# Four feed-forward layers of a model on one core: mixer outputs in the order 0, 4, 1, 5, ..., the seven products reordered, two token factors made inside the first pair

## The chip, the core and the metric

The kernel runs on one core of a Trainium2 chip. The core has a matrix engine (TensorE, "PE" in the profile; its weight loads are listed apart as "PEld"), a vector engine (VectorE, "DVE"), a scalar engine (ScalarE, "ACT"), a general engine (GpSimd, "POOL") and an engine that only issues transfers here (SyncE, "SP"). Each engine runs its own queue of instructions strictly from front to back; an instruction that waits for a semaphore holds up everything behind it in its queue. The metric is the device time of one execution in microseconds (us).

## The reference, cut to what matters

A block of four layers works on 512 tokens of width 1024, in float32. Each layer is a mixer (two state-space and gated-linear-attention halves, a latent attention, a retention, a stick-breaking attention) and then a feed-forward part with a hidden width of 2816 (22 x 128):

```python
x = x + mixer(rms_norm(x, mix_norm))            # four different mixers
x = x + swiglu(rms_norm(x, ffn_norm), w_gate, w_up, w_down)

def swiglu(h, w_gate, w_up, w_down):
    return (jax.nn.silu(h @ w_gate) * (h @ w_up)) @ w_down

def rms_norm(x, w):
    y = x * lax.rsqrt(jnp.mean(x * x, axis=-1, keepdims=True) + 1e-6)
    return y * w
```

The change touches the place where a mixer's output is added to x and the gate and up products of the following feed-forward part begin. There are four such places. They are called the first to the fourth place here.

## The kernel before, in words

x lies in SBUF transposed, as eight tiles of 128 features x 512 tokens, numbered m = 0 to 7. A float32 product is made of three passes: each operand is split into a high part rounded to the engine's fp32r type and a low remainder (`hh`/`hl` for x, `oh`/`ol` for combinations of x, `wh`/`wl` for weights), and high x high, high x low and low x high are accumulated in PSUM. The high part is made by ACT, the low part by DVE.

A mixer ends with its output projection. It makes one output tile m after the other in PSUM (`lin`), and `residual` adds it to tile m of x on DVE and then calls `norm_prep` for the next layer. The first and the third mixer use `out_a` (24 matmuls of 512 columns for each output and one weight piece of 128 x 1024), the second and the fourth `out_two` (12 matmuls for each output; one weight piece serves two outputs). Before the change the outputs come in the order 0, 1, ..., 7.

The feed-forward part computes gate and up with seven products in place of eight. The four weight blocks are b11, b12, b21, b22 (up and gate, for the tiles 0 to 3 and the tiles 4 to 7 of x), and the tokens are cut into two halves of 256. Product n multiplies one weight factor with one token factor (`self.opers[n]`, four entries k = 0 to 3, one for each tile of 128 features). Token factor 1 is the first half of the tiles 0 to 3, factors 2 and 3 are the two halves of the tiles 4 to 7; the factors 4 to 7 are sums and differences of these, so entry k of them needs tile k and tile k + 4. `operand` (line 433) makes them: for m below 4 a copy of x times the gain (`xg`) and the split; for m from 4 on another copy `xg`, four combinations `xo` of 256 columns on DVE (L210, L219), four roundings `oh` of 256 columns on ACT (L226) and four remainders `ol` of 256 columns on DVE. `norm_sq` squares the tile on ACT and adds it to a running sum `sq`, on POOL, or on DVE for m = 7.

`pair_seven` (line 625) then makes one pair of hidden tiles: seven products of 24 matmuls of 256 columns each (`seven`, line 612), in the order 1, 5, 6, 4, 2, 3, 7, and the additions, the scaling with the norm's factors `rbc` and the SiLU between them. It runs 11 times in each feed-forward part. The weight factors in the same order are b11, a = b11 + b12, a + b22, d = b12 + b22, b21, a + b21 (+ b22), b22. `wsum` makes a sum while it is loaded: SP loads one block into a buffer `ws`, and POOL issues a second transfer that adds the other block to it; a further block is added by DVE in place (`ws<-ws,wr`). Each of the three weight tags (`wr`, `ws` and the converted `wh`/`wl`) has three buffers of 128 x 1024. The norm's sum over features (a matmul with ones, then a Newton iteration on DVE in `ry`, `ra`, `rv`) and its broadcast (a matmul with `ident`) stand in a small queue `vq` that `fill` empties every other group of matmuls, so they fall among the first products of the first pair.

The code only says what depends on what and in which order it was written. The framework's scheduler fixes each engine's order when the program is built, and may put instructions of a later product between those of an earlier one. The order on each engine is therefore part of the change.

## Time and profile before

| what | value |
|---|---|
| median of 3 runs | 2796.18 us (2795.95 to 2799.39) |
| profiled execution | 2799.2 us, span of its trace 2797.1 us |
| PE busy | 98% of the span |
| DVE busy | 67% |
| ACT busy | 43% |
| POOL busy | 9% |
| mean granted clock of PE | 0.987 |
| data read from memory | 309.77 MB, 112 GB/s over the span |

PE is busy nearly all the time; the stretches where it is not, and those where its granted clock is below 1, are short. The profile's second part cuts the span into 40 slices and shows both: all slices have PE at 8 tenths or more, and the mean hides what happens within a slice of 70 us. The timeline and the sums over chosen stretches are needed for that.

### The profile page before, as it was taken

What the parts mean: (1) busy time and instruction counts of PE and PEld (TensorE: products, weight loads), DVE (VectorE), ACT (ScalarE), POOL (GpSimd) and SP (SyncE); (2) the same over time, 40 slices, a digit from 0 to 9 for tenths busy, and PEclk for the clock granted to TensorE, in tenths of its full rate; (3) what the DMA queues carried; (4) which work ended last, traced back from release to release, by engine and by line L of the source; (5) the groups of instructions that cost most, each with busy time, mean ns of one, the idle gap of its engine ahead of it and who ended that gap; (6) DMA issues with size and microseconds to landing.
All of it is one profiled execution on the core that took longest, in us unless ns stands there. A gap on an engine that the chain in (4) does not pass through costs nothing.

```text
span 2797.1 us, 40184 instructions
## 1 busy us (share of the span) xinstructions
PE 2729.5 (98%) x15989; PEld 2348.3 (84%) x15989; DVE 1873.2 (67%) x3020; ACT 1211.7 (43%) x1893; POOL 243.9 (9%) x230
## 2 busy tenths in 40 slices
PE   8999998999998999999999999999999999899999
PEld 6787768999876679998888888799988877699987
DVE  7466567888349977887345544678864388888852
ACT  5444334445226664444233333444442365644431
POOL 2011001000002110000000000100001011100000
PEclk9999998999999998999999999999999999999999
DMA  6232213766321115674332222267643211157632
GB/s 201 86 107 91 68 55 92 191 175 178 96 82 43 46 38 150 176 190 134 98 111 78 87 84 79 80 155 193 169 134 100 91 55 52 46 146 185 168 112 77
DMA packets 91739, 314.50 MB, mean 112 GB/s; under 512 B 10320, under 2 KB 12176, under 8 KB 91552
## 3 DMA queue, kind: packets, MB, share of 16 engines
q1 hardware_dynamic: 78880, 265.79, 29.6%
q0 software_dynamic: 12672, 46.14, 10.3%
q8 instruction: 126, 2.06, 0.3%
q14 instruction: 61, 0.50, 0.1%
HBM read 309.77 MB, written 2.13 MB: 112 GB/s over the span
## 4 chain that ended last, share of the span: by engine, by line
PE 60%; DVE 4%; ACT 1%; issue 1%; POOL 0%; DVEq 0%; ACTq 0%; POOLq 0%
PE lin L229 45%; PE mx L229 14%; PE mx L233 1%; DVE P L1503 1%; DVE wl L210 1%; DVE beta L210 0%; ACT wh L226 0%; DVE hl L219 0%; DVE xo L210 0%; DVE ol L210 0%; DVE x L210 0%; DVE ws L210 0%; POOL sq L210 0%; DVE xo L219 0%; ACT oh L226 0%
## 5 line engine op out<-in xcount | busy, mean ns | idle before, releaser
L226 ACT ACTIVATE wh<-wr 128x1024 fp32r<-128x1024 f32 (+2 forms) x411 | 423.0, 1033 | 824.5 <-PE lin L229 391.6
L210 DVE TENSOR_TENSOR wl<-wr,wh 128x1024 fp32r<-128x1024 f32 (+2 forms) x411 | 491.8, 1198 | 415.9 <-ACT wh L226 415.1
L229 PE MATMUL lin<-hh,wh 128*128 128x512 f32 (+1 forms) x1432 | 491.0, 344 | 7.4 <-ACT wh L226 7.3
L229 PE MATMUL lin<-hl,wh 128*128 128x512 f32 (+1 forms) x1432 | 486.6, 340 | 0.8 <-DVE hl L219 0.8
L229 PE MATMUL lin<-hh,wl 128*128 128x512 f32 (+1 forms) x1432 | 485.6, 339 | 0.8 <-DVE wl L210 0.8
L229 PE MATMUL lin<-oh,wh 128*128 128x256 f32 x1056 | 306.2, 290 | 23.8 <-ACT oh L226 23.5
L229 PE MATMUL lin<-ol,wh 128*128 128x256 f32 x1056 | 306.1, 290 | 4.8 <-DVE ol L210 4.6
L229 PEld LDWEIGHTS lin<-hh,wh 128*128 128x128 f32 x1432 | 271.6, 190 | 43.6 <-issue 7.6
L229 PE MATMUL lin<-oh,wl 128*128 128x256 f32 x1056 | 305.1, 289 | 0.4 <-DVE wl L210 0.3
L229 PEld LDWEIGHTS lin<-hl,wh 128*128 128x128 f32 x1432 | 271.6, 190 | 31.9 <-DVE hl L219 3.5
L229 PEld LDWEIGHTS lin<-hh,wl 128*128 128x128 f32 x1432 | 271.5, 190 | 32.0 <-DVE wl L210 2.0
L226 ACT ACTIVATE wh<-ws 128x1024 fp32r<-128x1024 f32 x176 | 185.6, 1056 | 253.4 <-DVE ws L210 126.2
L229 PE MATMUL lin<-fh,wh 128*128 128x512 f32 x704 | 274.3, 390 | 0.0
L229 PE MATMUL lin<-fl,wh 128*128 128x512 f32 x704 | 273.9, 389 | 0.0
L229 PE MATMUL lin<-fh,wl 128*128 128x512 f32 x704 | 273.8, 390 | 0.0
L229 PEld LDWEIGHTS lin<-oh,wh 128*128 128x128 f32 x1056 | 207.8, 197 | 27.1 <-ACT oh L226 26.9
L210 DVE TENSOR_TENSOR wl<-ws,wh 128x1024 fp32r<-128x1024 f32 x176 | 215.1, 1224 | 21.9 <-ACT wh L226 21.9
L229 PE MATMUL lin<-wh,hh 128*128 128x512 f32 (+1 forms) x560 | 224.8, 402 | 0.8 <-ACT v L226 0.7
L229 PE MATMUL lin<-wh,hl 128*128 128x512 f32 (+1 forms) x560 | 217.7, 389 | 0.0
L229 PE MATMUL lin<-wl,hh 128*128 128x512 f32 (+1 forms) x560 | 216.7, 387 | 0.0
L229 PEld LDWEIGHTS lin<-ol,wh 128*128 128x128 f32 x1056 | 208.5, 197 | 6.7 <-DVE ol L210 6.7
L229 PEld LDWEIGHTS lin<-oh,wl 128*128 128x128 f32 x1056 | 208.7, 198 | 1.1 <-DVE wl L210 1.0
(297 smaller groups left out, 4967.6 us busy)
## 6 DMA issues: line engine op xcount, KB each, us to landing
wr<-in_wgu_dram SPq DMA_DIRECT2D x132, 512.0 KB, 4.3
ws<-in_wgu_dram SPq DMA_DIRECT2D x88, 512.0 KB, 4.3
ws<-in_wgu_dram POOLq DMA_DIRECT2D x88, 512.0 KB, 7.4
wr<-in_wd_dram SPq DMA_DIRECT2D x64, 512.0 KB, 3.6
wr<-in_wo_dram SPq DMA_DIRECT2D x48, 512.0 KB, 3.5
wr<-in_w3b_dram SPq DMA_DIRECT2D x32, 512.0 KB, 3.5
wr<-in_w1b_dram SPq DMA_DIRECT2D x24, 512.0 KB, 3.7
wr<-in_wd_dram SPq DMA_DIRECT2D x32, 384.0 KB, 3.2
```

What stands on the lines that cost most here:

```text
L210: (eng or self.nc.vector).tensor_tensor(out=out, in0=a, in1=b, op=op)
L226: self.nc.scalar.activation(out, a, f, **k)
L229: self.last = self.nc.tensor.matmul(out, lhsT, rhs, start=start, stop=stop, **k)
L233: self.nc.tensor.transpose(out, in_, self.ident[0:n, 0:n])
L1503: self.nc.vector.tensor_tensor_scan(P[:, 0:ke - 1][:, ::-1], d, d, 1.0, op0=ALU.mult, op1=ALU.bypass)
```

## The change

Three things change together. First, all mixers write their outputs in the order of `PAIRS`, and the weight pieces are loaded (and for `out_two` packed) in that order, so tile k + 4 follows tile k at once. Second, `operand` builds the factors otherwise. The copy `xg` is made for m below 4 only. Factors 4 and 5 are made in one tile of 512 columns, with one rounding `oh` and one remainder `ol` for both; their signs are turned, and the additions in `pair_seven` become subtractions. Factors 6 and 7 are made the same way by a function `late`: in the first and the third feed-forward part (`EARLY`) at once, but for m = 7, and else inside the first pair, behind products 1 and 4. Third, the products run in the order 1, 4, 2, 5, 6, 3, 7, with the weight factors in the order b11, d, b21, a, a + b22, a + b22 + b21, b22; the transfers of a summed factor are issued one job ahead (`joblist`). The copy of product 1 (`u2`) now stands between products 1 and 2, which accumulate into the same PSUM tile X. Product 6's tile Y moves from the pool `lin` (3 buffers) to the pool `mx` (5 buffers). The norm's sum is written behind product 5 and its broadcast behind product 3 of the first pair.

```diff
+PAIRS = (0, 4, 1, 5, 2, 6, 3, 7)
+EARLY = ("ffn1", "ffn3")
...
-                yield from (A["wo1"][i, m] for i in range(2) for m in range(8))
+                yield from (A["wo1"][i, m] for i in range(2) for m in PAIRS)
...
-        return [first, second, third, fourth, lambda: st["b21"], lambda: (st["a"], None, plus("b21")),
-                lambda: st["b22"]]
+        return [(put("b11", lambda: self.wraw(b11)), None),
+                (lambda: (st["d"], None, None), put("d", lambda: self.wsum(b12, b22))),
+                (put("b21", lambda: self.wraw(b21)), None),
+                (lambda: (st["a"], None, None), put("a", lambda: self.wsum(b11, b12))),
+                (fifth, None),
+                (lambda: (st["a"], None, plus("b21")), None),
+                (lambda: st["b22"], None)]
...
     def operand(self, m, gain):
+        if m == 0:
+            self.opers = {n: [None] * 4 for n in range(1, 8)}
+            self.xas, self.late = [None] * 4, deque()
+        k = m % 4
+        x, g = self.x[:, m, :], self.col(gain, m)
         own = lambda o: tuple(a[:, o:o + 256] for a in self.h[m])
...
+        def halves(t, n, scale):
+            hi, lo = [self.T2(F32R, name=f) for f in ("oh", "ol")]
+            self.act(hi, t, AF.Copy, scale=scale)
+            self.stt(lo, t, scale, hi.bitcast(F32), ALU.mult, ALU.subtract)
+            for i in range(2):
+                self.opers[n + i][k] = tuple(a[:, 256 * i:256 * i + 256] for a in (hi, lo))
+
         if m < 4:
...
-            def parts(n):
-                if k % 2 == 0:
-                    self.ot[n] = [self.T2(F32R, name=f) for f in ("oh", "ol")]
-                hi, lo = [a[:, 256 * (k % 2):256 * (k % 2) + 256] for a in self.ot[n]]
-                self.act(hi, o[n], AF.Copy)
-                self.tt(lo, o[n], hi.bitcast(F32), ALU.subtract)
-                self.opers[n].append((hi, lo))
...
+            xa = self.xas[k] = self.T2(name="xg")
+            self.act(xa, x, AF.Copy, scale=g)
+            self.h[m] = self.split(x, g)
+            self.opers[1][k] = own(0)
+            return
+        xa = self.xas[k]
+        self.h[m] = self.split(x, g)
+        self.opers[2][k] = own(0)
+        self.opers[3][k] = own(256)
+        t = self.T2(name="xo")
+        self.tt(t[:, 0:256], xa[:, 0:256], xa[:, 256:512], ALU.subtract)
+        self.stt(t[:, 256:512], x[:, 256:512], g, xa[:, 256:512], ALU.mult, ALU.subtract)
+        halves(t, 4, -1.0)
+
+        def late():
+            r = self.T2(name="xo")
+            self.stt(r[:, 0:256], t[:, 256:512], -1.0, xa[:, 0:256], ALU.mult, ALU.subtract)
+            self.stt(r[:, 256:512], x[:, 0:256], g, r[:, 0:256], ALU.mult, ALU.add)
+            halves(r, 6, 1.0)
+
+        self.late.append(late)
+        if gain in EARLY and m < 7:
+            self.late.popleft()()
...
+    def pair_seven(self, first):
+        X, Z, C, Y, W = self.LIN(), self.MX(), self.LIN(), self.MX(), self.MX()
...
         self.seven(X, 1, True, True)
-        self.seven(C, 5, True, True)
-        self.seven(Y, 6, True, True)
...
         self.act(u2, X, AF.Copy)
+        late(2)
+        self.seven(Z, 4, True, True)
+        late(2)
+        self.seven(X, 2, False, True)
+        self.seven(C, 5, True, True)
+        if first:
+            self.norm_sums()
+        self.seven(Y, 6, True, True)
         self.add(u2, Y, u2)
-        self.seven(Z, 4, True, True)
...
-        self.add(u3, Z, u2)
+        self.tt(u3, u2, Z, ALU.subtract)
...
-        self.add(g2, C, u3)
-        self.seven(X, 2, False, True)
-        self.row_scales()
+        self.tt(g2, C, u3, ALU.subtract)
+        self.seven(W, 3, True, True)
+        if first:
+            self.norm_bcast()
...
     def out_a(self, w, hs, gain):
-        for m in range(8):
+        for m in PAIRS:
...
-                self.residual(2 * mp + i, ps, gain)
+                self.residual(mp + 4 * i, ps, gain)
```

What this does to the engines' queues is seen at three places. The first is the queue of DVE at the first place, from the addition of the last output, m = 7 (`x<-lin`), on. `wl` is a converted weight factor, `ws<-ws,wr` the addition of a weight block, `hl` the low part of a tile of x, `xo` the combinations and `ol` their remainders. Before:

```order
L210 TENSOR_TENSOR x<-lin_3514,x 128x512
L210 TENSOR_TENSOR ol_3499<-xo_3486,oh_3498 128x256
L210 TENSOR_TENSOR wl_3627<-ws_3400,wh_3626 128x1024
L219 SCALAR_TENSOR_TENSOR hl_3503<-x,cols,hh_3502 128x512
L210 TENSOR_TENSOR ol_3508<-xo_3486,oh_3507 128x256
L210 TENSOR_TENSOR ws_3400<-ws_3400,wr_3579 128x1024
L210 TENSOR_TENSOR wl_3663<-ws_3519,wh_3662 128x1024
L210 TENSOR_TENSOR xo_3549<-xg_3547,xg_3321 128x256
L210 TENSOR_TENSOR xo_3550<-xg_3321 128x256
L219 SCALAR_TENSOR_TENSOR xo_3549<-xo_3549,xg_3321 128x256
L219 SCALAR_TENSOR_TENSOR hl_3561<-x,cols,hh_3560 128x512
L210 TENSOR_TENSOR ol_3489<-xo_3549,oh_3488 128x256
```

And after:

```order
L212 TENSOR_TENSOR x<-lin_3490,x 128x512
L212 TENSOR_TENSOR wl_3584<-wr_3498,wh_3583 128x1024
L221 SCALAR_TENSOR_TENSOR hl_3526<-x,cols,hh_3525 128x512
L212 TENSOR_TENSOR xo_3529<-xg_3481 128x256
L221 SCALAR_TENSOR_TENSOR xo_3529<-x,cols,xg_3481 128x256
L212 TENSOR_TENSOR wl_3614<-ws_3495,wh_3613 128x1024
L221 SCALAR_TENSOR_TENSOR ol_3533<-xo_3529,oh_3532 128x512
L221 SCALAR_TENSOR_TENSOR xo_3576<-xo_3529,xg_3481 128x256
L212 TENSOR_TENSOR sq_3205<-sq_3205,sq_3536 128x512
```

Before, ten rows stand between the addition of output 7 and the first `ol` of its entry k = 3 (factor 5), three of them rows of 1024 columns for weights and six that make other factors of tiles 6 and 7. After, five rows stand there, two of them for weights, and the combination that needs only tile 3 (`xo<-xg`) and the one that needs tile 7 give factors 4 and 5 in one `ol`.

The second is DVE at the second place (`out_two`), again from the addition of the last output on. Before:

```order
L210 TENSOR_TENSOR x<-lin_9884,x 128x512
L210 TENSOR_TENSOR wl_9978<-ws_9695,wh_9977 128x1024
L210 TENSOR_TENSOR xo_9811<-xg_9809,xg_9680 128x256
L210 TENSOR_TENSOR xo_9812<-xg_9680 128x256
L219 SCALAR_TENSOR_TENSOR xo_9811<-xo_9811,xg_9680 128x256
L210 TENSOR_TENSOR ws_9695<-ws_9695,wr_9930 128x1024
L210 TENSOR_TENSOR ol_9770<-xo_9811,oh_9769 128x256
L210 TENSOR_TENSOR ol_9775<-xo_9811,oh_9774 128x256
L210 TENSOR_TENSOR ol_9780<-xo_9812,oh_9779 128x256
L219 SCALAR_TENSOR_TENSOR hl_9823<-x,cols,hh_9822 128x512
L219 SCALAR_TENSOR_TENSOR xo_9812<-xo_9811,xg_9809 128x256
L210 TENSOR_TENSOR wl_10014<-ws_9836,wh_10013 128x1024
```

And after:

```order
L212 TENSOR_TENSOR x<-lin_9817,x 128x512
L212 TENSOR_TENSOR wl_9897<-wr_9792,wh_9896 128x1024
L221 SCALAR_TENSOR_TENSOR ol_9779<-xo_9775,oh_9778 128x512
L221 SCALAR_TENSOR_TENSOR hl_9811<-x,cols,hh_9810 128x512
L221 SCALAR_TENSOR_TENSOR hl_9832<-x,cols,hh_9831 128x512
L212 TENSOR_TENSOR xo_9835<-xg_9808 128x256
L221 SCALAR_TENSOR_TENSOR xo_9835<-x,cols,xg_9808 128x256
L212 TENSOR_TENSOR wl_9941<-ws_9789,wh_9940 128x1024
L221 SCALAR_TENSOR_TENSOR ol_9839<-xo_9835,oh_9838 128x512
L221 SCALAR_TENSOR_TENSOR xo_9882<-xo_9660,xg_9634 128x256
L212 TENSOR_TENSOR sq_9640<-sq_9640,sq_9842 128x512
L221 SCALAR_TENSOR_TENSOR xo_9882<-x,cols,xo_9882 128x256
```

Before, the queue still holds the combinations of tiles 5, 6 and 7 there, and 25 rows stand between the addition of output 7 and the `ol` of its entry for product 5. After, seven stand ahead of the `ol` for products 4 and 5: it holds a remainder of tile 6, the low parts of tiles 3 and 7 (`hl`), the combinations of tile 7 for factors 4 and 5, two converted weights, and only then the four `late` combinations for factors 6 and 7, whose weight factor (`ws<-ws,wr`) is added between them.

The third is ACT around the start of a pair late in the first feed-forward part (`wh` is a converted weight block or factor, `u<-lin` the copy of product 1 out of PSUM, `g<-g` and `u<-u` are the SiLUs of the pair before). Before:

```order
L226 ACTIVATE wh_12060<-ws_11957 128x1024
L226 ACTIVATE wh_12090<-ws_11957 128x1024
L226 ACTIVATE u_2300_11915<-u_2300_11915 128x512
L226 ACTIVATE wh_12119<-ws_12023 128x1024
L226 ACTIVATE u_2329_12149<-lin_12055 128x512
L226 ACTIVATE wh_12152<-wr_12064 128x1024
L226 ACTIVATE wh_12184<-ws_11957 128x1024
L226 ACTIVATE wh_12220<-wr_11990 128x1024
L226 ACTIVATE wh_12253<-wr_12189 128x1024
```

And after:

```order
L228 ACTIVATE wh_12044<-wr_11976 128x1024
L228 ACTIVATE u_2287_11808<-u_2287_11808 128x512
L228 ACTIVATE wh_12074<-ws_11973 128x1024
L228 ACTIVATE u_2316_12042<-lin_12007 128x512
L228 ACTIVATE wh_12102<-ws_11973 128x1024
L228 ACTIVATE wh_12131<-ws_11973 128x1024
L228 ACTIVATE wh_12170<-wr_12048 128x1024
L228 ACTIVATE wh_12203<-wr_12139 128x1024
```

In both the copy of product 1 stands directly behind one conversion of a summed factor (before that of d, after that of a), which its two transfers must have filled. What moved is the reader behind it: product 2, which overwrites the copied tile, follows product 1 by one product (4) where it followed by three (5, 6, 4).

## Rows read from the trace of the kernel before

**Rows 1.** The page's first part: busy time of the matmul engine, share, instructions.

```profile
PE 2729.5 (98%) x15989; PEld 2348.3 (84%) x15989; DVE 1873.2 (67%) x3020; ACT 1211.7 (43%) x1893; POOL 243.9 (9%) x230
```

**Rows 2.** Waits of PE: who ended them, us in total, times, longest.

```profile
PE lin L229 <- ACT oh L226: 23.5, 10, 5.2
...
PE mx L229 <- DVE ry L219: 5.8, 3, 2.8
```

**Rows 3.** Busy time by stretch: start:end, length, engines' busy us, granted clock, DMA.

```profile
442.93:470.66 27.73, 20.34 (x114) 19.26 (x113) 17.04 (x38) 10.56 (x18) 6.57 (x3) 0.69 0.34 80
1039.40:1070.01 30.61, 20.45 (x113) 18.65 (x112) 24.60 (x49) 15.53 (x28) 8.94 (x4) 0.67 0.24 58
1802.33:1829.51 27.18, 20.17 (x115) 18.90 (x114) 17.03 (x38) 10.59 (x19) 6.56 (x3) 0.75 0.32 80
2430.64:2461.10 30.46, 20.29 (x113) 17.87 (x112) 25.09 (x51) 16.50 (x30) 7.21 (x4) 0.72 0.23 56
1093.21:1113.38 20.17, 20.17 (x171) 20.17 (x170) 16.66 (x21) 8.96 (x11) 1.71 (x2) 1.00 0.73 183
421.17:442.93 21.76, 21.76 (x97) 18.02 (x96) 18.13 (x29) 13.51 (x23) 5.11 (x3) 1.00 0.23 73
1028.52:1039.40 10.88, 10.88 (x49) 9.01 (x48) 9.91 (x17) 6.64 (x12) 2.73 (x2) 1.00 0.15 48
```

**Rows 4.** PE in order of time, first and fourth place: start, us, instruction, idle before.

```profile
451.50 0.38 PE L229 MATMUL lin<-oh,wh 128*128 128x256 f32 x1 [2.96 <-ACT oh L226]
...
454.11 0.41 PE L229 MATMUL lin<-oh,wl 128*128 128x256 f32 x1
454.33 0.41 PE L229 MATMUL lin<-oh,wh 128*128 128x256 f32 x1
...
2457.27 1.13 PE L229 MATMUL mx<-ident,ry 128*128 128x128 f32 x8 [0.17 <-DVE ry L219]
2458.16 0.36 PE L229 MATMUL mx<-oh,wh 128*128 128x256 f32 x1
```

**Rows 5.** DVE in order of time, first place.

```profile
445.23 0.69 DVE L210 TENSOR_TENSOR x<-lin,x 128x512 f32<-128x512 f32 x1
...
447.30 0.75 DVE L219 SCALAR_TENSOR_TENSOR hl<-x,cols,hh 128x512 fp32r<-128x512 f32 x1
...
448.30 1.22 DVE L210 TENSOR_TENSOR ws<-ws,wr 128x1024 f32<-128x1024 f32 x1
449.44 1.22 DVE L210 TENSOR_TENSOR wl<-ws,wh 128x1024 fp32r<-128x1024 f32 x1
450.57 0.42 DVE L210 TENSOR_TENSOR xo<-xg,xg 128x256 f32<-128x256 f32 x1
...
451.58 1.77 DVE L219 SCALAR_TENSOR_TENSOR hl<-x,cols,hh 128x512 fp32r<-128x512 f32 x1
453.27 1.08 DVE L210 TENSOR_TENSOR ol<-xo,oh 128x256 fp32r<-128x256 f32 x3
...
459.23 0.16 DVE L219 SCALAR_TENSOR_TENSOR ra<-ry 128x4 f32<-128x4 f32 x1
```

**Rows 6.** POOL in order of time, first place.

```profile
447.98 4.82 POOL L210 TENSOR_TENSOR sq<-sq,sq 128x512 f32<-128x512 f32 x1 [7.80 <-ACT sq L226]
```

**Rows 7.** POOL by line and shape: count, busy us, mean ns, idle before.

```profile
L210 POOL TENSOR_TENSOR sq<-sq,sq 128x512 f32<-128x512 f32 x51 | 87.7, 1719 | 1004.3 <-ACT sq L226 930.2 <-PE lin L229 73.7
```

**Rows 8.** ACT in order of time, first place and a later pair.

```profile
448.35 0.71 ACT L226 ACTIVATE hh<-x,cols 128x512 fp32r<-128x512 f32 x1
...
1101.98 1.04 ACT L226 ACTIVATE wh<-ws 128x1024 fp32r<-128x1024 f32 x1
1102.93 0.58 ACT L226 ACTIVATE u<-lin 128x512 f32<-128x512 f32 x1
```

**Rows 9.** DMA issues of the weights: count, KB each, median us to landing.

```profile
ws<-in_wgu_dram SPq DMA_DIRECT2D x88, 512.0 KB, 4.3
ws<-in_wgu_dram POOLq DMA_DIRECT2D x88, 512.0 KB, 7.4
```

More of the change, by code (lines that the diff above doesn't have):

```diff
@@ L328, in plan @@
                     yield from (A["w3b"][2 * hd + i, j] for i in range(2) for j in range(4))
-                yield from (A["wo3"][i, m] for i in range(2) for m in range(8))
+                yield from (A["wo3"][i, m] for i in range(2) for m in PAIRS)
             elif l == "L4":
@@ L333, in plan, with joblist @@
                 yield from (A["wo4"][i, m] for i in range(2) for m in range(4))
-    def wload(self):
-        if not self.jobs:
-            ap = next(self.pieces, None)
-            if ap is None:
-                return
-            if isinstance(ap, tuple):
-                self.jobs.extend(self.factors(ap[1]))
-            else:
-                self.jobs.append(lambda: self.wraw(ap))
-        job = self.jobs.popleft()()
+    def joblist(self, layers):
+        jobs = []
+        for ap in self.plan(layers):
+            if isinstance(ap, tuple):
+                jobs += self.factors(ap[1])
+            else:
+                jobs.append((lambda ap=ap: self.wraw(ap), None))
+        for i, (_, early) in enumerate(jobs):
+            if i == 0 and early:
+                early()
+            if i + 1 < len(jobs) and jobs[i + 1][1]:
+                jobs[i + 1][1]()
+            yield jobs[i][0]()
+    def wload(self):
+        job = next(self.jobs, None)
         if job is not None:
@@ L364, in factors, with put, g @@
         st = {}
+        def put(n, f):
+            def g():
+                st[n] = f()
+                return st[n]
+            return g
         def plus(n):
@@ L371, in plus, with fifth @@
             return f
-        def first():
-            st["b11"] = self.wraw(b11)
-            st["a"] = self.wsum(b11, b12)
-            return st["b11"]
-        def second():
+        def fifth():
             st["b22"] = self.wraw(b22)
-            return st["a"], None, None
-        def third():
-            st["d"] = self.wsum(b12, b22)
             return st["a"], None, plus("b22")
-        def fourth():
-            st["b21"] = self.wraw(b21)
-            return st["d"], None, None
-        return [first, second, third, fourth, lambda: st["b21"], lambda: (st["a"], None, plus("b21")),
-                lambda: st["b22"]]
+        return [(put("b11", lambda: self.wraw(b11)), None),
[5 more added lines that the diff above has]
+                (lambda: st["b22"], None)]
     def wconv(self):
@@ L426, in norm_prep @@
     def norm_prep(self, m, gain):
-        if gain not in self.gain_ffn:
-            self.h.append(self.split(self.x[:, m, :], self.col(gain, m)))
+        if gain in self.gain_ffn:
+            self.operand(m, gain)
         else:
-            self.operand(m, gain)
+            self.h[m] = self.split(self.x[:, m, :], self.col(gain, m))
         self.norm_sq(m)
     def operand(self, m, gain):
-        own = lambda o: tuple(a[:, o:o + 256] for a in self.h[m])
-        if m == 0:
-            self.opers = {n: [] for n in range(1, 8)}
-            self.xas, self.ot = [], {}
@@ L622, in seven, with late @@
                 self.mm(out, wl[:, s], xh, False, z, skip_group_check=True)
-                self.fill()
-    def pair_seven(self):
-        X, C, Y, Z, W = self.LIN(), self.LIN(), self.LIN(), self.MX(), self.MX()
+    def pair_seven(self, first):
+        X, Z, C, Y, W = self.LIN(), self.MX(), self.LIN(), self.MX(), self.MX()
         v = lambda a: a.rearrange("p (i n) -> p i n", i=2)
         rb = lambda o: self.rbc[:, o:o + 256].unsqueeze(1).to_broadcast([128, 2, 256])
+        def late(n):
+            for _ in range(n):
+                if self.late:
+                    self.late.popleft()()
         self.seven(X, 1, True, True)
-        self.seven(C, 5, True, True)
-        self.seven(Y, 6, True, True)
         ts = [self.T2(name="f") for _ in range(2)]
@@ L649, in pair_seven @@
         self.seven(C, 7, False, True)
-        self.add(u2, C, u2)
+        self.tt(u2, C, u2, ALU.subtract)
         self.mul(v(u2), v(u2), rb(0))
-        self.act(u2, u2, AF.Silu, scale=-1.0)
+        self.act(u2, u2, AF.Silu)
         for i in range(2):
```

52 lines of the change are left out of this document (15 added, 37 removed).

## Prediction

> **What bounds the kernel now.** I read the page's first part, then the waits of PE, then sums over chosen stretches, then the timelines of the engines in one of them. PE is busy for 98% of the span, 2729.5 of 2797.1 us [rows 1], so the kernel is bound by PE, and what PE does not spend on work is small. Nearly half of it has one name: PE waited 23.5 us for `oh`, the rounded combinations of x, in 10 waits of up to 5.2 us, and 5.8 us for `ry`, the norm's iteration [rows 2]. Both lie at the four places where a mixer hands over to the feed-forward part.
>
> The stretches of [rows 3] show what a place costs. In each row the length stands behind the two times; then come the busy times of PE, its weight loads, DVE, ACT and POOL with their counts, and the granted clock. The first four reach from the first matmul of product 1 to the first one behind the fourth product. The fifth is one whole later pair: seven products in 20.17 us, PE busy throughout, clock 1.00, so 2.88 us for a product and 0.12 us for a matmul. Four products are 11.5 us. The norm's broadcast takes 0.9 us at the full clock (from 2457.27 to 2458.16 [rows 4]); I put the norm's sum, of as many rows, at the same. A place without a wait would last 13.3 us. The four last 27.73, 30.61, 27.18 and 30.46 us, so they lose 14.4, 17.3, 13.9 and 17.2 us, together 62.8 us. This is all that the change can win there.
>
> The loss has two halves. At the first place PE stands still 2.96 us for `oh` at 451.50 and after that starts a matmul every 0.21 us (454.11, 454.33) where it needs 0.12 [rows 4]. The granted clock of these stretches is 0.67 to 0.75 in the mean [rows 3], a mix of 2.4 GHz and the lower level of 1.2 GHz, and it fell each time after such waits. A wait that goes takes its share of the slow matmuls with it.
>
> What ends last in the wait is DVE. At the first place the last output is added at 445.23, and the `ol` of its entry for product 5 starts only at 453.27 [rows 5]. The ten rows between them (the first order block of the change) explain it. A DVE row that another follows at once starts the next one 0.09 us before its own end (449.44 behind 448.30 + 1.22, 450.57 behind 449.44 + 1.22), so 256 columns cost 0.34, the addition of an output 0.60, `hl` 0.66 and 1024 columns 1.13. The sum is 0.60 + 2 x 0.34 + 2 x 0.66 + 3 x 1.13 + 3 x 0.34 = 7.0 us; the one `hl` at 451.58 took 1.77 in place of 0.75, which adds 1.0 and gives 8.0, as the trace has it.
>
> **The change part by part.** *Work.* At each place ACT has 12 rows less: four copies `xg`, and eight roundings of 512 columns for sixteen of 256. DVE has eight rows less, but not less time: sixteen `ol` of 256 columns are 16 x 0.34 = 5.4 us, eight of 512 are 8 x 0.66 = 5.3, if they cost what `hl` does, the nearest row (the trace has no remainder of 512 columns of a combination). So nothing is saved; all gain must come from what stands ahead of what.
>
> *First and third place.* Each output is 5.44 us of PE there (21.76 for four [rows 3]), so DVE has caught up when output 7 comes. From its addition to the `ol` of the fourth entry of factors 4 and 5 the order now has 0.60 + 1.13 + 0.66 + 2 x 0.34 + 1.13 = 4.2 us. The addition starts some 0.2 us after product 1 does, so this `ol` ends 5.2 us after it (0.75 for its own row). PE's order puts 41 matmuls ahead of its first use, 24 of product 1, 10 of product 4 and 7 of product 5, or 4.9 us. The wait is 0.3 us, and 1.3 if a POOL addition strikes as at 451.58. I take 1.2, as in the row. `oh` comes earlier: ACT has a conversion and `hh` (0.71 [rows 8]) ahead of it, and both run beside the DVE rows counted. The gain is 13.2 and 12.7 us. If this cover failed and the clock fell as before, some 6 us would remain of each.
>
> *Second and fourth place.* Here an output is only 2.72 us (10.88 for four), and DVE is busy for 9.91 us of these 10.88 and 24.60 of the 30.61 behind them [rows 3]: it is DVE that binds. From the addition of output 7 to the `ol` for products 4 and 5 the new order has 0.60 + 1.13 + 0.66 + 2 x 0.66 + 2 x 0.34 + 1.13 = 5.5 us; it ends 6.5 us after product 1 starts, against 4.9 of PE: 1.6 us. To the last `late` remainder follow eight combinations, four remainders, one sum of squares, three conversions, two additions of weights and eleven small rows of the iteration at some 0.2 (0.16 in [rows 5] and its hand-over): 2.7 + 2.6 + 0.6 + 3.4 + 2.3 + 2.2 = 13.8 us, against 89 matmuls and the norm's sum, 11.6 us of PE: 2.2 more. That is 3.8 us with nothing late. But two outputs now give DVE 2 x 0.60 + 2 x 0.66 + 0.68 + 0.66 + 2 x 1.13 = 6.1 us for 5.44 of PE, and POOL adds a tile for each of the first seven outputs, at 1.0 us to DVE where it strikes. A lag of 1 to 4 us when product 1 starts, one or two strikes behind it, and a stretch at the lower clock after waits of this size add to the 3.8. The loss is 3.8 at least and today's 17 at most; I take 10, nearer to the counted rows with strikes than to either end. The gain is 7.3 and 7.2 us.
>
> *POOL's additions.* The row at 447.98 took 4.82 us where the mean is 1.72 [rows 6, 7], and the DVE row at 451.58 beside its end took 1.0 us too much [rows 5]: each holds up the other. The Trainium skill, in "SBUF — State Buffer", section "Who interferes with whom", says that a DVE instruction with two SBUF inputs and a GpSimd instruction that reads SBUF exclude each other, and the second waits for the whole of the first. By that rule each strike would cost DVE up to a whole addition, 1.72 us and not 1.0; with one strike at the first and third place and three at the others the gain would shrink by 0.7 x 8 = 5.6 us.
>
> *The norm.* Its sum now stands behind product 5 and its broadcast behind product 6 in PE's order, more than 5 us apart, so the waits for `ry` (5.8 us, part of the losses above) should go.
>
> *The eleven pairs of each layer.* Products, additions and conversions are as many as before. DVE is busy for 16.66 of 20.17 us, ACT for 8.96 [rows 3], and PE covers both. The summed factor needs two transfers in a row, 4.3 and 7.4 us [rows 9]; two of them a pair in three buffers leave each buffer 30 us, and a holds one for 11.7 us and three products. I cost this, the other order of the weights on SP's queue, and POOL's queue behind it at nothing; without that cover each microsecond would count 44 times.
>
> *Sum.* 13.2 + 7.3 + 12.7 + 7.2 = 40.4 us. The profiled execution took 2799.2 us (span 2797.1), so it becomes 2758.8. It lies 3.0 us above the median of the runs shown, so the median becomes 2755.8.
>
> **The rivals.** *All waits go (12%).* DVE catches up at the second and fourth place too, 3.8 us stay there and 0.3 at the others: the gain is 62.8 - 8.2 = 54.6, 2742 us. For it: fewer instructions, evenly spread. Against it: the 24.60 us of DVE there.
>
> *The clock stays low (20%).* Short waits keep the lower clock: 6 us stay at the first and third place and 13 to 17 at the others. The gain is 17 to 25, the time 2771 to 2779 us. For it: at the second place the rows of PE fell to the lower clock after waits too, and waits of 1 to 2 us remain. Against it: at the first place too little is left to wait for.
>
> *Product 2 waits for the copy of product 1 (3%).* It writes the tile that ACT must first copy, and now has only product 4, 2.88 us, as cover. The copy takes 0.58 us and stands behind a conversion of 1.04 [rows 8], so it ends at the latest some 1.6 us after product 1, 1.2 us in time, if the conversion can start. If a's second transfer came later than that, each microsecond would cost 44 us. From 0.9 us a pair on, the gain is gone; at 1.5 us the time is 2822. Against it: a's transfers are issued products ahead.
>
> *The scheduler leaves the order (2%).* Then 2796 stays; the order blocks speak against it.
>
> **How the numbers follow.** The forecast, 2748 to 2764 us on its own, has 63%. The range from 2742 to 2775 holds it, all but the lower edge of the first rival and a good half of the second. A measurement of this kernel tells 0.2%, 5.6 us, from no change. Faster by more than that: the forecast and the first two rivals, 95%. Within it: the scheduler's 2%. Slower: the copy's 3%.
>
> **What would show it.** In the profile after, the first and third place should last 13 to 16 us at a clock near 1.00, with no wait over 1.3 us, and the second and fourth 19 to 25, with several waits of about 1 us for `oh` and `ol` and DVE without idle time. The waits for `ry` should be gone, and a pair should last 20.17 us. A pair that is longer, or a wait of PE for `u`, would show the copy's rival; a first place above 18 us, the clock's.

## The result, and the profile after

| | kernel before | changed kernel |
|---|---|---|
| median (4 runs each) | 2797.78 us (2795.95 to 2800.47) | 2762.64 us (2760.17 to 2763.06) |
| ratio, 95% interval | 1 | 0.9872 (0.9855 to 0.9889) |
| span of the profiled execution | 2797.1 us | 2760.6 us |

The change saves 35.1 us. The forecast was a gain of 40.4 and 2755.8 us, so it is right in kind, 6.8 us too low in time, and inside its own range (2748 to 2764).

The page's first line after stands against [rows 1]; the columns are the same. PE is busy 11 us less and the span is 36.5 us shorter, so 25 us of the gain are idle time of PE. Of the 11 us some 6 are the clock: of the first 300 matmuls of gate and up at each place, about 120 in all stood in unbroken rows 0.21 us apart before, and about 50 do after. The rest of the 11 us was not followed up.

```profile
PE 2718.4 (98%) x15989; PEld 2337.7 (85%) x15989; DVE 1869.1 (68%) x2988; ACT 1203.1 (44%) x1845; POOL 233.2 (8%) x230
```

The waits of PE in the changed kernel (releaser, us in total, times, longest) answer [rows 2]. `oh`, 23.5 us before, is 1.8; `ry`, 5.8 before, is gone; no wait for `u`, the copy of product 1, appears. Of the first line one wait of 7.3 us stood there before.

```profile
PE lin L231 <- ACT wh L228: 9.4, 3, 7.4
PE mx L231 <- DVE sqk L212: 3.9, 1, 3.9
PE mx L231 <- DVE ol L221: 2.8, 4, 1.3
...
PE mx L231 <- DVE wl L212: 2.0, 2, 1.0
PE lin L231 <- DVE hl L221: 2.0, 3, 1.4
...
PE mx L231 <- ACT oh L228: 1.8, 2, 1.6
```

Sums over stretches of the changed kernel, columns as in [rows 3]: the four places from the first matmul of product 1 to the first of product 4 in the second pair, which is eight products, the norm's sum and its broadcast (8 x 2.88 + 1.8 = 24.84 us without a wait), and then, behind the second place, the stretch from there to the first of product 4 in the third pair.

```profile
443.13:469.32 26.19, 25.81 (x210) 25.09 (x209) 21.03 (x37) 12.66 (x15) 2.11 (x3) 1.00 0.53 134
1027.36:1063.40 36.04, 30.44 (x209) 28.64 (x208) 29.88 (x52) 17.22 (x24) 4.87 (x5) 0.86 0.42 116
1784.41:1810.58 26.17, 25.79 (x209) 25.07 (x208) 21.02 (x37) 12.18 (x15) 2.09 (x3) 1.00 0.51 128
2400.40:2436.27 35.87, 30.54 (x210) 28.46 (x209) 29.52 (x53) 17.58 (x25) 6.30 (x5) 0.86 0.40 111
1063.40:1083.55 20.15, 20.15 (x168) 19.95 (x167) 17.18 (x22) 9.78 (x11) 1.72 (x2) 1.00 0.58 141
```

The places lose 1.35, 11.2, 1.33 and 11.0 us, 24.9 together, where they lost 62.8. That is 37.9 us; the span shows 36.5. The missing 1.4 us lie mostly in the later pairs. By the PE timeline, from first matmul to first matmul, the second pair of each layer takes 20.35 to 20.51 us in place of 20.16, 1.0 us in all, and the third to the tenth take 20.17 to 20.19 in place of 20.16, 0.6 us in all. The first and third place are nearly free, at the full clock. The second and fourth still lose 11 us, partly at the lower level (the granted clock is 0.86 in their stretches).

What ends last at the first place is seen on three engines. On PE in order of time (start, us, instruction, idle before), the first matmuls of product 5 stand among those of product 4, and one of them waits for a converted weight:

```profile
447.25 0.39 PE L231 MATMUL lin<-oh,wh 128*128 128x256 f32 x1
447.47 0.28 PE L231 MATMUL lin<-ol,wh 128*128 128x256 f32 x1
447.76 0.38 PE L231 MATMUL mx<-oh,wh 128*128 128x256 f32 x1
448.51 0.39 PE L231 MATMUL lin<-oh,wl 128*128 128x256 f32 x1 [0.36 <-DVE wl L212]
```

The conversion that it waits for, that of a (ACT, then DVE with the `ol` of the fourth entry behind it):

```profile
446.13 1.06 ACT L228 ACTIVATE wh<-ws 128x1024 fp32r<-128x1024 f32 x1 [1.31 <-issue]
...
447.23 1.23 DVE L212 TENSOR_TENSOR wl<-ws,wh 128x1024 fp32r<-128x1024 f32 x1 [0.36 <-ACT wh L228]
448.37 0.69 DVE L221 SCALAR_TENSOR_TENSOR ol<-xo,oh 128x512 fp32r<-128x512 f32 x1
```

ACT starts it at 446.13, when product 1 has ended (its last matmul starts at 445.88). The trace names no releaser; by the program the instruction waits for PE, since of the three buffers of `wh` it takes the one that held b11, the factor of product 1. Experiment e7 tests that. The `ol` ends at 449.06, just ahead of its first use at 449.20.

At the second place the waits come one behind the other, and then the clock falls (12 matmuls 0.21 us apart from 1033.65 on, and 16 more from 1039.24 to 1042.66):

```profile
1029.56 0.38 PE L231 MATMUL mx<-oh,wh 128*128 128x256 f32 x1 [0.25 <-ACT oh L228]
1031.23 0.39 PE L231 MATMUL mx<-ol,wh 128*128 128x256 f32 x1 [1.29 <-DVE ol L221]
...
1033.27 0.58 PE L231 MATMUL lin<-hl,wh 128*128 128x256 f32 x1 [1.42 <-DVE hl L221]
1033.65 0.41 PE L231 MATMUL lin<-hh,wl 128*128 128x256 f32 x1
1033.86 0.41 PE L231 MATMUL lin<-hh,wh 128*128 128x256 f32 x1
...
1037.60 0.58 PE L231 MATMUL lin<-oh,wh 128*128 128x256 f32 x1 [0.98 <-ACT wh L228]
...
1050.99 0.38 PE L231 MATMUL mx<-hh,wl 128*128 128x256 f32 x1 [1.01 <-DVE wl L212]
```

POOL's additions and DVE's rows there:

```profile
1018.75 1.75 POOL L212 TENSOR_TENSOR sq<-sq,sq 128x512 f32<-128x512 f32 x1 [1.47 <-ACT sq L228]
...
1025.81 1.75 POOL L212 TENSOR_TENSOR sq<-sq,sq 128x512 f32<-128x512 f32 x1 [1.40 <-ACT sq L228]
...
1031.08 3.26 POOL L212 TENSOR_TENSOR sq<-sq,sq 128x512 f32<-128x512 f32 x2
...
1019.27 1.78 DVE L221 SCALAR_TENSOR_TENSOR hl<-x,cols,hh 128x512 fp32r<-128x512 f32 x1
...
1026.32 0.68 DVE L212 TENSOR_TENSOR x<-lin,x 128x512 f32<-128x512 f32 x1
1026.92 1.19 DVE L221 SCALAR_TENSOR_TENSOR hl<-x,cols,hh 128x512 fp32r<-128x512 f32 x1
...
1031.29 3.61 DVE L221 SCALAR_TENSOR_TENSOR hl<-x,cols,hh 128x512 fp32r<-128x512 f32 x2
```

Three times an `hl` that starts inside a POOL addition ends 0.55 us after it (1021.05 behind 1020.50, 1028.11 behind 1027.56, 1034.90 behind 1034.34): it does its work only when POOL is done. The addition of an output at 1026.32, whose one input lies in PSUM, runs inside a POOL addition at its usual 0.68. The four `hl` took 3.6 us more than 0.75 each.

The wait for the buffer is at the second place too, and there it stops DVE. Product 1 ends late, behind these `hl`; ACT stands idle until the conversion of a can start, and DVE behind it:

```profile
1036.49 1.06 ACT L228 ACTIVATE wh<-ws 128x1024 fp32r<-128x1024 f32 x1 [4.11 <-issue]
1037.58 1.23 DVE L212 TENSOR_TENSOR wl<-ws,wh 128x1024 fp32r<-128x1024 f32 x1 [1.96 <-ACT wh L228]
```

So the prediction's sign "DVE without idle time" did not come: a part of the loss there is DVE waiting for a weight (1.96 us at the fourth place as well).

### The profile page after: what moved, and what is told of

It reads as the page before. It is cut to its first block, busy times and chain, and to the rows that moved or that the text cites. A ratio compares the mean times of both kernels' runs of the same rounds, so it can differ in the third digit from the quotient of the medians.

```text
span 2760.6 us, 40043 instructions
## 1 busy us (share of the span) xinstructions
PE 2718.4 (98%) x15989; PEld 2337.7 (85%) x15989; DVE 1869.1 (68%) x2988; ACT 1203.1 (44%) x1845; POOL 233.2 (8%) x230
## 5 line engine op out<-in xcount | busy, mean ns | idle before, releaser
L231 PE MATMUL lin<-oh,wh 128*128 128x256 f32 x704 | 202.4, 287 | 2.0 <-ACT wh L228 2.0
L231 PE MATMUL mx<-ol,wh 128*128 128x256 f32 x704 | 200.7, 285 | 2.8 <-DVE ol L221 2.8
L231 PE MATMUL mx<-oh,wh 128*128 128x256 f32 x704 | 201.4, 286 | 2.0 <-ACT oh L228 1.8
L231 PE MATMUL lin<-oh,wl 128*128 128x256 f32 x704 | 200.1, 284 | 1.0 <-DVE wl L212 1.0
L231 PE MATMUL mx<-oh,wl 128*128 128x256 f32 x704 | 200.1, 284 | 0.0
L231 PE MATMUL lin<-ol,wh 128*128 128x256 f32 x704 | 199.5, 283 | 0.0
```

The lines of the kernel that those rows point to most:

```text
L231: self.last = self.nc.tensor.matmul(out, lhsT, rhs, start=start, stop=stop, **k)
```

## The experiments

For every kernel the loss of a place is counted in one way: from the first matmul of product 1 to the 301st matmul of gate and up, less 300 x 0.12 and 1.8 us for the norm (from the PE timeline of one profile of each; the last section shows that the second and fourth place of one and the same kernel differ by some 1.5 us between two profiles). All ratios are to the kernel before in the same call.

| kernel | median us | ratio (95%) | 1st | 2nd | 3rd | 4th | sum |
|---|---|---|---|---|---|---|---|
| before | 2797.78 | 1 | 14.4 | 17.3 | 13.7 | 17.1 | 62.5 |
| changed | 2762.64 | 0.9872 (0.9855 to 0.9889) | 1.5 | 11.5 | 1.3 | 11.3 | 25.5 |
| changed, again (e9) | 2764.50 | 0.9869 (0.9855 to 0.9884) | 1.5 | 11.1 | 1.4 | 11.3 | 25.3 |
| before + order of outputs (b1) | 2792.07 | 0.9977 (0.9967 to 0.9987) | 6.9 | 18.3 | 6.7 | 20.7 | 52.6 |
| without the order of outputs (e1) | 2778.68 | 0.9920 (0.9903 to 0.9936) | 8.3 | 12.2 | 7.8 | 12.6 | 40.9 |
| without the order of products (e2) | 2764.61 | 0.9872 (0.9857 to 0.9886) | 1.0 | 10.1 | 1.0 | 14.9 | 27.0 |
| without the norm's position (n1) | 2770.25 | 0.9890 (0.9874 to 0.9907) | 5.4 | 12.5 | 2.6 | 13.0 | 33.5 |
| EARLY empty (e3) | 2766.78 | 0.9878 (0.9864 to 0.9893) | 3.7 | 11.0 | 3.4 | 11.5 | 29.6 |
| EARLY all four (e4) | 2775.17 | 0.9908 (0.9893 to 0.9922) | 1.5 | 15.9 | 1.4 | 18.5 | 37.2 |
| squares added on DVE (e5) | 2760.85 | 0.9864 (0.9850 to 0.9879) | 1.5 | 7.6 | 1.4 | 12.9 | 23.4 |
| the same, again (e10) | 2761.84 | 0.9861 (0.9846 to 0.9876) | 1.5 | 9.1 | 1.4 | 11.5 | 23.4 |
| squares not added (e6) | 2760.49 | 0.9859 (0.9844 to 0.9874) | 1.5 | 8.9 | 1.4 | 9.6 | 21.3 |
| and less DVE (e8) | 2750.09 | 0.9819 (0.9804 to 0.9834) | 0.5 | 4.2 | 0.2 | 6.8 | 11.6 |
| four buffers (e7) | 2869.79 | 1.0251 (1.0227 to 1.0275) | 2.3 | 10.2 | 0.8 | 11.0 | 24.2 |

**e1, the order of the outputs undone.**

```diff
-PAIRS = (0, 4, 1, 5, 2, 6, 3, 7)
+PAIRS = (0, 1, 2, 3, 4, 5, 6, 7)
...
-                self.residual(mp + 4 * i, ps, gain)
+                self.residual(2 * mp + i, ps, gain)
```

(and the weights of `out_two` packed to match).

> Undone alone: the mixers write their outputs in the order 0 to 7 again. My theory (a place costs what stands ahead of the last entries in DVE's queue): at the first and third place an output takes PE 5.44 us and DVE needs about 5.1 us for each of the last four, so these places stay within 1 us of their 1.3 us. At the second and fourth the last four outputs cost DVE about 3.2 us each for 2.72 us of PE, 2 to 4 us more at each: 2767 to 2771 us. Rival (the order of the outputs is most of the change's gain): every place goes back by about half of what it won, 2778 us or more. Rival (the order gives nothing, since DVE's total is the same): 2763 us.

Measured: 2778.68 us, 16 more than the changed kernel (13 by the ratios), as the first rival had it in size; but neither it nor my theory named the places. The first and third lose 6.8 and 6.5 us more, the second and fourth only 0.7 and 1.3. DVE's rows at the first place show why:

```profile
444.00 0.68 DVE L212 TENSOR_TENSOR x<-lin,x 128x512 f32<-128x512 f32 x1
...
446.34 0.41 DVE L221 SCALAR_TENSOR_TENSOR xo<-xo,xg 128x256 f32<-128x256 f32 x1
446.78 0.49 DVE L221 SCALAR_TENSOR_TENSOR xo<-x,cols,xo 128x256 f32<-128x256 f32 x1
...
448.92 2.30 DVE L212 TENSOR_TENSOR ws<-ws,wr 128x1024 f32<-128x1024 f32 x1
451.15 0.74 DVE L221 SCALAR_TENSOR_TENSOR hl<-x,cols,hh 128x512 fp32r<-128x512 f32 x1
```

Between output 7 (444.00) and its `hl` (451.15) now stand the rows of tile 6, which comes directly ahead of it and is a tile with combinations too, and three weight rows, one of them an addition (2.30 us in place of 1.22) that started inside a POOL addition (448.61 to 450.14). With pairs, tile 3 stands there, which makes none. I had weighed rates (5.1 us of DVE for 5.44 of PE) and not what stands ahead of the last tile.

**b1, the order alone on the kernel before.** The same edit in the other direction.

> The kernel before with the outputs in the order 0, 4, 1, 5, ... and nothing else of the change. If the parts add up (undoing the order in the changed kernel cost 16 us of its 37), the order alone is worth about 16 us of the kernel before: 2783 us where before is 2798. If the order pays only together with the merged operand, because before ten DVE rows stand behind the last output whatever its order: under 5 us, 2793 us or more. If the order is nearly all of the change: 2770 us or less.

Measured: 2792.07 us, a ratio of 0.9977: some 6 us, near the second of the three cases. By the places it gives 7.5 and 7.0 us at the first and third, a little more than e1 took (6.8 and 6.5), and takes 1.0 and 3.6 at the others. So the order of the outputs is worth 7 us at each place where an output is long, and adds to the rest there; at the other two it helps nothing by itself. (The time moved some 3 us less than the sum of the places; the fourth mixer, ahead of the fourth place, is 2.9 us longer in this profile.) The wait that is left at the first place is the norm's, 14 matmuls behind its sum:

```profile
458.23 1.31 PE L230 MATMUL mx<-ident,ry 128*128 128x128 f32 x8 [4.09 <-DVE ry L220]
```

**e2, the order of the products undone** (with the weight factors; the late combinations all ahead of product 5).

```diff
-        self.seven(Z, 4, True, True)
-        late(2)
-        self.seven(X, 2, False, True)
+        late(4)
         self.seven(C, 5, True, True)
...
+        self.seven(Z, 4, True, True)
+        self.seven(X, 2, False, True)
```

> Undone alone: the products run in the order 1, 5, 6, 4, 2, 3, 7 again, with their weight factors, and all late combinations stand ahead of product 5. My theory: product 6 is now behind 48 matmuls and needs factor 6, for which DVE works 13.8 us behind the last output at the second and fourth place: some 6 us more there and 1 to 2 us at the first and third, 2776 us. Rival (the merged operand and the order of the outputs did it, the order of the products is worth nothing): 2763 us. Rival (the order of the products is the whole gain): 2795 us or more.

Measured: 2764.61 us, the rival's 2763 within the spread of the runs; the places lose 0.3 to 1.4 us less at three and 3.6 more at the fourth. The order of the products, the part that gives an entry more matmuls of cover, is worth nothing that these runs can tell. (With it undone the pairs from the third to the tenth are back at 20.16 us.)

**n1, the norm's position undone.**

```diff
-        if first:
-            self.norm_sums()
...
-        if first:
-            self.norm_bcast()
+        self.row_scales()
```

with `norm_finish` and `fill` as before.

> Undone alone: the norm's sum and its broadcast stand in the queue that is emptied every other group of matmuls again, as before the change. Theory (the waits for ry, 5.8 us in the kernel before and 15.6 us in the kernel with the order of the outputs alone, go because sum and broadcast stand further apart): a wait for ry of 2 to 4 us comes back at each of the four places, 8 to 16 us in all: 2771 to 2779 us. Rival (with the merged operand DVE is free in time, and the position of the norm is worth nothing): within 3 us of 2763.

Measured: 2770.25 us, just under the theory's 2771, and for another reason: no wait for `ry` came back. The edit did not undo what it was meant to. The scheduler put 32 to 58 matmuls of 256 columns between the norm's sum and its broadcast, where the kernel before has 14 at the first and third place and b1 14 to 17, and where the changed kernel has 72 and 48. Over all of these: behind 14 to 17 matmuls PE waited 2.8 to 4.1 us, behind 20 under 0.2, and behind 32 and more not at all (0.28 once, in e2). DVE's iteration in b1, from 452.58 on, shows what such a gap has to cover, since conversions stand among its small rows:

```profile
452.58 0.16 DVE L224 TENSOR_SCALAR rv<-mx 128x4 f32<-128x4 f32 x1
452.65 1.22 DVE L211 TENSOR_TENSOR wl<-wr,wh 128x1024 fp32r<-128x1024 f32 x1
...
455.21 1.23 DVE L211 TENSOR_TENSOR wl<-ws,wh 128x1024 fp32r<-128x1024 f32 x1 [1.06 <-ACT wh L227]
456.35 0.15 DVE L220 SCALAR_TENSOR_TENSOR ra<-ry 128x4 f32<-128x4 f32 x1
```

What n1 lost, it lost elsewhere: the scheduler now put product 5 ahead of product 4, and PE waits 1.08 and 0.76 us for its converted weight at the first and the third place. The price of the norm's position by itself stays open.

**e3 and e4, which places make the late combinations early.**

```diff
-EARLY = ("ffn1", "ffn3")
+EARLY = ()
```

and with all four names in e4.

> EARLY is empty: at the first and third place too the combinations for factors 6 and 7 of all four tiles are made inside the first pair, 4.0 us more of DVE behind the last output. My theory: they end before the 89th matmul, so nothing is lost: 2763 us, the places at 1.3 us. Rival (DVE is the bound of every place): 2 to 4 us more at each of the two, 2767 to 2771 us.

> EARLY holds all four layers: at the second and fourth place three of the four late combinations move ahead of the last output. My theory (DVE binds there, and the entries of factors 4 and 5 come first): 4 us of DVE rows move ahead of the first wait, so each of the two places loses 3 to 6 us more: 2769 to 2775 us. Rival (only DVE's sum up to product 6 counts): 2763 us. Rival (the waits there come from POOL's additions and from converted weights, not from DVE's rows): within 2 us of 2763.

Measured: e3 2766.78 us, 2.2 us more at each of the two places, the lower end of the rival: my 89 matmuls of cover had no 4 us to spare. (At the first place PE now also waits 0.64 us for a converted weight, at 460.41, and 0.36 for an `ol`, at 464.42.) e4 2775.17 us, 4.4 and 7.2 us more at the second and fourth place, at the upper edge of my theory (2769 to 2775 us, 3 to 6 us each): rows of DVE ahead of the last output count there.

**e5 and e6, POOL's additions of squares.**

```diff
-            self.add(self.acc, self.acc, sq, None if m == 7 else self.nc.gpsimd)
+            self.add(self.acc, self.acc, sq, None if m == 7 or gain in self.gain_ffn else self.nc.gpsimd)
```

That is e5; e6 keeps the addition for m = 7 alone:

```diff
-        else:
+        elif m == 7 or gain not in self.gain_ffn:
```

> The changed kernel with all additions of squares of the four places on DVE, none on POOL: 0.60 us each, six more at a place, 3.6 us. In the changed kernel the hl rows beside POOL's additions at the second place took 1.78, 1.19 and 3.61 (two rows) where 0.75 each is normal, 3.6 us too much together. Theory (DVE waits out POOL's additions, and its queue is what binds at the second and fourth place): the two sums cancel, within 3 us of 2763. Rival (the long rows lie off the path, DVE's own rows bind): 3 to 6 us more at each of the two places, 2769 to 2775. Rival (an addition on POOL costs far more than its row, since it also takes the clock down): 2757 or less.

> The changed kernel with the additions of squares of tiles 1 to 6 left out at the four places (the norm's sum is then that of tiles 0 and 7 alone). Theory (POOL's additions hold DVE up and DVE's queue binds): the 3.6 us of long rows at the second and fourth place go, with the slow matmuls behind the waits 3 to 6 us each, 2751 to 2757 us; the first and third place stay at 1.3 us. Rival (what binds there is the converted weight, which waits for a buffer): within 2 us of 2763.

Measured: e5 2760.85 us, the sums cancel as expected. e6 2760.49 us, above the 2751 to 2757 of the theory and, with its places at 8.9 and 9.6, below the rival's "nothing" by 2.6 and 1.7 us. POOL's additions are a part of the loss, not most of it: some 2 us a place by these profiles, with an uncertainty of nearly that size, and about 3 us in all by the ratios.

**e8, DVE relieved.** As e6, and the low parts of tiles 4 to 7 are not made:

```diff
-        self.h[m] = self.split(x, g)
+        hi = self.T2(F32R, name="hh")
+        self.act(hi, x, AF.Copy, scale=g)
+        self.h[m] = hi, self.h[k][1]
```

> The changed kernel without the additions of squares of tiles 1 to 6 and without the low parts hl of tiles 4 to 7 at the four places (products 2 and 3 take the low parts of tiles 0 to 3 in their place): 2.6 us of DVE rows and POOL's additions gone, matmuls, conversions and roundings as before. Theory (DVE's queue binds the second and fourth place, with POOL's additions as a part of it): their loss of 11.4 us falls to 4 to 6 us, the first and third place to under 1 us: 2749 to 2753 us. Rival (the converted weights, or ACT, bind there once POOL is out of the way): no lower than the kernel without the squares, about 2758 us.

Measured: 2750.09 us, inside the theory's 2749 to 2753; 10 us less than e6 for 4 x 2.6 us of DVE rows. This is the run that names what bounds the second and fourth place in the main: the work in DVE's queue. It does not remove the wait for the buffer: at the second place DVE still stands 1.19 us for the conversion of a. The second place is the clean case, since PE's order there is nearly that of the changed kernel (8.9 us in e6, 4.2 here); at the other three the scheduler also moved product 5 behind product 2. The sums over the same places, columns as above, hold at least as many matmuls (the counts in brackets) in 28.87 and 32.19 us as the changed kernel did in 36.04 and 35.87, and the clock is 1.00 at the second:

```profile
443.22:469.00 25.78, 25.78 (x215) 25.64 (x214) 20.93 (x37) 13.28 (x16) 1.75 (x2) 1.00 0.53 141
1026.13:1055.00 28.87, 27.01 (x211) 25.44 (x210) 25.01 (x47) 15.29 (x21) 1.75 (x2) 1.00 0.51 128
2392.81:2425.00 32.19, 28.71 (x215) 27.29 (x213) 26.90 (x50) 18.32 (x26) 1.75 (x2) 0.95 0.46 115
```

**e7, four buffers for the converted weights.**

```diff
-        t = self.wp.tile([128, 1024], F32, tag="ws", name=self.nm("ws"))
+        t = self.wp.tile([128, 1024], F32, tag="ws", bufs=2, name=self.nm("ws"))
...
+            hi = self.wp.tile([128, 1024], F32R, tag="wh", bufs=4, name=self.nm("wh"))
+            lo = self.wp.tile([128, 1024], F32R, tag="wl", bufs=4, name=self.nm("wl"))
```

(and 14 small tiles of 64 columns in place of 20).

> The changed kernel with four buffers in place of three for the converted weights wh and wl (and, to make room, two for the summed raw weights ws and 14 in place of 20 small tiles). In the changed kernel the conversion of a, the factor of product 5, starts when product 1 ends (446.13 behind 445.88 at the first place, 1036.49 behind 1036.21 at the second), since it waits for the buffer of b11. Theory (this wait sets the stop of PE behind the first matmuls of product 5): the first and third place lose under 0.5 us in place of 1.3, the second and fourth lose 2 to 4 us less: 2753 to 2758 us. Rival (DVE's queue binds, a conversion made earlier only changes places with other rows): 2761 to 2765 us. Rival (the two buffers for ws hold up the transfers in the pairs): a pair longer than 20.17 us, 2770 us or more.

Measured: 2869.79 us. The second rival came true, and the places themselves bear out the first theory only where DVE does not bind: the third has no wait at all (0.8 us in place of 1.3; the first's 2.3 hold 1.5 of the new wait), the second and fourth stay within 1.3 us. But at these two the fourth buffer did not take the wait away, it moved it: a is converted early, and now the conversion of a + b22 stands until product 1 has ended (1065.41 at the second place), with DVE idle for 2.90 and 2.98 us. What the wait for a buffer costs at the second and fourth place is therefore not shown. What the two buffers for `ws` cost is the rival of the prediction that had 3%. ACT in a pair of the first feed-forward part:

```profile
603.24 1.06 ACT L228 ACTIVATE wh<-ws 128x1024 fp32r<-128x1024 f32 x1 [6.76 <-DMA ws<-in_wgu_dram]
604.21 0.61 ACT L228 ACTIVATE u<-u 128x512 f32<-128x512 f32 x1
604.73 0.58 ACT L228 ACTIVATE u<-lin 128x512 f32<-128x512 f32 x1
```

and the first matmul of product 2 behind it, with the sum of these waits over the kernel:

```profile
605.36 0.38 PE L231 MATMUL lin<-hh,wh 128*128 128x256 f32 x1 [1.91 <-ACT u L228]
```

```profile
PE lin L231 <- ACT u L228: 45.6, 30, 4.4
```

A summed factor that arrives late holds its conversion, the conversion holds the copy of product 1 behind it in ACT's queue, and product 2 waits for the copy. With three buffers for `ws` no wait for `u` appears: it is covered there. (e7 changes three counts of buffers at once; that it is `ws` is read from the DMA wait in the first line. Another 35.5 us of e7 are waits for `g`, an addition of the pair before.)

**e9 and e10, side by side.**

> The changed kernel once more, beside the next one on the same chip: 0.987 of the kernel before, as measured.

> The kernel with all additions of squares of the places on DVE once more, timed beside the changed kernel on the same chip. If moving them off POOL is a gain: 1 to 4 us under the changed kernel in the medians of the same call. If the earlier 2 us were noise: within 1 us of it, on either side.

Measured: 2764.50 us (2762.40 to 2765.11) and 2761.84 us (2759.85 to 2763.61). With e5 (2.2 us by the ratios) this is 2 to 3 us for the additions on DVE, the same sign twice, but the ranges overlap; it is a likely gain of 0.1%, not a shown one. Both profiles of this version put the sum of the places at 23.4 us, 2 less than the changed kernel's.

## Why the prediction was right, and where its steps failed

- *Where the time is.* Right: the four places lost 62.8 us and lose 24.9. (One reading was off: `oh` was called nearly half of PE's idle time, and its 23.5 us are a third of 67.6.)
- *First and third place.* The term was 1.2 us each, measured 1.35 and 1.33, so their gain of 13.2 and 12.7 us came. The reason given was wrong, and that the number fits is luck: 1.2 was 0.3 and nearly one whole strike of a POOL addition, and none struck there. What PE waits for is the conversion of a, which waits for a buffer. The scheduler's order has product 5 behind only nine matmuls of product 4. The step counted the rows of the weights on DVE but not DVE's waits for ACT's conversions: from the addition of output 7 (443.33) to the fourth `ol` (448.37) it took 5.0 us in place of 4.2, 0.58 of it such waits. With the fourth buffer of e7 the third place loses 0.8 us and no wait is left in the first pair of either. In e8 they lose 0.5 and 0.2, but the later place of product 5 there by itself gives the conversion time.
- *Second and fourth place.* The term was 10 us each, measured 11.2 and 11.0; this is the term that was mis-sized. That DVE's work sets most of it is what e8 shows at the second place and e4 supports; that DVE would have no idle time was wrong (1.96 us for the conversion of a). Of the loss of 11.5 at the second place the waits of PE are 5.5 us in all, and 28 matmuls at 0.21 in place of 0.12 are 2.5; the rest is spacing around the waits. I had counted 3.8 without strikes and chosen 10 between bounds; the choice was good, but its parts were not worked out, so its nearness is in part luck.
- *The signs.* Up to the first matmul behind the fourth product the places last 12.68, 20.50, 12.69 and 20.30 us, where 13 to 16 and 19 to 25 were named; the norm's sum, which the 13 held, now lies behind that point.
- *POOL's additions.* Priced at 1.0 us for a strike, with one to two behind the lag. Measured at the second place: 3.6 us in four `hl`. A struck row takes what is left of POOL's addition and then 0.55 of its own. The row that I took as a price was one such overlap, not the most that one can cost. The rule of the Trainium skill ("SBUF — State Buffer", "Who interferes with whom") that I had weighed, two SBUF inputs excluded for the whole of the other's instruction, agrees with the three ends at 0.55 us, and its exception for a DVE instruction with one SBUF input with the 0.68 at 1026.32.
- *The norm.* The waits for `ry` went, and the distance on PE is the reason as far as the counts above go.
- *The eleven pairs.* Put at nothing; they cost 1.6 us (1.0 in the second pairs, 0.6 in the third to tenth). The cover that I named for the copy is the right one: e7 takes it away and the kernel becomes 105 us slower than the changed one.
- *The 5.3 us by which it is off* (40.4 against 35.1): 2.5 are the places (24.9 left where the terms leave 22.4), 1.4 lie in the span outside them, mostly in the pairs, and 1.4 between spans and medians (36.5 and 35.1). The last is no more than what executions differ by: the start of the first place alone is 443.13 us in one profile of the changed kernel and 445.24 in the other.
- *What each part is worth.* The order of the outputs: 7 us at the first and third place, by removal and by addition alike; at the others about 1 us by removal and nothing by addition. The order of the products: none. The norm's position could not be undone by itself, since the scheduler chose another order. The split between early and late: 2.2 us at each of the first and third place against none early (e3), 4.4 and 7.2 at the others against all early (e4). The merged operand was not run alone. Without the order of the outputs (e1) the places still lose 21.6 us less than before, more than half of the gain; this is what the merged operand, the split and the norm's position give together, and their shares stay open.

## What to carry to other kernels

When a queue that trails the bound engine must finish the last of several tiles, look at which tile stands ahead of it: putting a cheap tile before the last expensive one was worth 7 us at two of the four places here, while more cover on the bound engine's side was worth none. Before calling a wait harmless, name the buffer count that hides it and try one fewer: a wait that cost nothing with three buffers appeared 30 times in 44 pairs with two. And ask what frees the buffer that a weight's conversion writes: here the end of the first product did, and at two of the four places ACT and DVE stood still until then.

## What the runs showed of the hardware that I had not expected

The same waits can bring the clock down or not. In n1 the first and the third place have the same two waits, 1.08 and 0.76 us, at the same instructions, and these sums from product 1 to product 3:

```profile
443.40:464.96 21.56, 19.72 (x138) 19.31 (x137) 14.80 (x28) 8.66 (x11) 1.25 (x2) 0.84 0.26 53
1789.81:1808.62 18.81, 16.90 (x137) 16.32 (x136) 14.88 (x28) 8.66 (x11) 1.23 (x2) 1.00 0.30 68
```

PE, DVE and ACT do the same in both, and in the 20 us ahead PE was busy throughout, at a granted clock of 1.00, in both. Then the clock is 0.50 at the first place (from 449.2 to 454.0), the lower level of 1.2 GHz, and 1.00 at the third (from 1795.6 to 1800.4). Over the stretches it is 0.84 and 1.00, and the first is 2.75 us longer: 23 matmuls of 256 columns, and those of the norm's sum, 0.21 us apart. The two runs of the version with the squares on DVE show it from execution to execution: no unbroken row of slow matmuls at the second place and 26 matmuls in such rows at the fourth in one (losses 7.6 and 12.9 us), 15 and 12 in the other (9.1 and 11.5), with the same sum of losses. A place with waits of this size therefore carries an uncertainty of some 1.5 to 3 us that no order of instructions explains.
